# Two half loads of the first row block, and earlier turns of the second and third block, in a hybrid decoder layer

## The chip, the cores and the metric

The kernel runs on one core of one Trainium2 chip. The metric is the time of one execution on the device in microseconds (us), as the median of several runs. The engines are named as the profile names them: PE (TensorE, matrix products and transposes), PEld (its weight loads), DVE (VectorE), ACT (ScalarE), POOL (GpSimd) and SP (SyncE, which issues nearly all DMAs here).

## The reference

One decoder layer on `x` of 1024 rows by 1024 columns, in float32. The part that matters here is its very beginning: a normalised `x`, with a gain for each column, times a wide matrix `w_in`.

```python
h = rmsnorm(x, mix_pre_norm[layer])          # x * rsqrt(mean(x*x) + eps) * gain
proj = h @ w_in[layer]                       # 1024 x 1024 by 1024 x 3584
q_a, k_a, v_a, q_h, f_h, i_h, g_h = jnp.split(proj, splits, axis=-1)
...                                          # dilated attention, HGRN2 recurrence
mixed = jnp.concatenate([attn, rec], axis=-1) @ w_out[layer]
x = x + rmsnorm(mixed, mix_post_norm[layer])
h = rmsnorm(x, mlp_pre_norm[layer])
ff = jnp.square(jax.nn.relu(h @ w_ff1[layer])) @ w_ff2[layer]
x = x + rmsnorm(ff, mlp_post_norm[layer])
```

## The kernel before, in words

The rows of `x` are cut into eight blocks of 128 rows (`xrows[0]` to `xrows[7]`, tile `xr`), and its columns into eight pieces of 128 (`k` = 0 to 7). A product needs the transpose of each block, so each piece is *turned*. `x_turn(t0, n, k)` (lines 281 to 288) lets PE transpose piece `k` of `n` blocks into a PSUM bank (tile `xt`), ACT write the scaled result as the high part (tile `hTh`, line 287), and DVE write the rest that the high part has lost (tile `hTl`, line 288). The banks of the turns go round in a ring of four (two of tag `t`, two of tag `s`): a turn can only begin when DVE has read the turn four places before it.

Weights come in the same two parts. `first_half(i, c)` (line 315) splits half `c` (512 of 1024 columns) of the raw weights `raws[i]`: ACT writes the high part (`wig0h`, line 86), DVE the low part (`wig0l`, line 87). A product is three matrix products: high by high, high by low, low by high. The first products of the kernel use `raws[0]` and `raws[1]` together, since each product is 256 columns wide, 128 from either.

The stretch that the change touches is lines 333 to 369, an order written out by hand; every engine keeps to it.

1. `keep_warm` (line 307) multiplies zeros on PE while nothing has been loaded.
2. The eight turns of block 0 (`x_turn(0, 1, k)`), with small products of zeros between them. In ACT's and DVE's order, `first_half(0, 0)` stands behind turn 3, `first_half(1, 0)` behind turn 5, and `first_half(0, 1)` and `first_half(1, 1)` behind turn 7.
3. `x_firsts(0)`: the products of block 0 for `k` = 0 to 3 (eight with the high weights, then four with the low weights; helper `x_first`, line 321).
4. Four turns of block 1; then `x_firsts(1)`, the products of block 0 for `k` = 4 to 7.
5. A loop over the groups of blocks (1), (2,3), (4,5), (6), (7), in which the products of one group (`x_mm`, line 290) and the turns of the next alternate. `LAG` says how many turns of a group are left for the loop in which they are needed themselves.

All loads of this stretch are issued by SP in program order: block 0 of `x`, `raws[0]`, `raws[1]`, blocks 1 to 7 of `x`, two small tables, and from there each further weight block when its buffer is free. Behind the loop, ACT and DVE write out the products of the last groups (`ig_evac`), split two more weight blocks (`wh`, `wl`) and prepare masks, while PE begins the products `pm_q` and `pm_f`. From there a queue of pieces of work with written-out costs fills PE; nothing in that part is changed.

Of the kernel before, what the change touches and what calls it, by code (L numbers as in the profile page):

```python
# [17 lines left out]
P = 128  # L18
T = 1024
D = 1024  # L20
NK = D // P
# [11 lines left out]
def f32(ap):  # L33
    return ap.bitcast(F32)
# [3 lines left out]
def hymba_layer(ctx, tc, x, w_in, w_out, w_ff1, w_ff2, g_pre, lb_logits, g_mix, g_post,  # L38
                g_mlp, g_mlp_post, bias_tab, level_masks, ident_in, fold_in, out):
    nc = tc.nc  # L40
# [11 lines left out]
    def slab(tag, name, dtype=F32, shape=(P, T)):  # L52
        return sp.tile(list(shape), dtype, tag=tag, name=name,
                       bufs={"S": 9, "T": 9, "P": 3, "BT": 2, "V8": 2, "R": 1}[tag])

    def bank(tag, name):
        return ps.tile([P, 512], F32, tag=tag, name=name,
                       bufs={"mm": 2, "s": 2, "t": 2, "pv": 2}[tag])
# [21 lines left out]
    def rsqrt_mean(dst, ssum, n, width):  # L80
        t = col("ms", width)
        G.tensor_scalar(t, ssum, 1.0 / n, EPS, op0=ALU.mult, op1=ALU.add)
        G.tensor_tensor(out=dst, in0=t, in1=nhalf[:, :width], op=ALU.pow)
# [26 lines left out]
    def w_split(eng=V):  # L110
        i = done[1]
        if i < len(stream):
            if done[0] <= i:
                w_load()
            hl = stream[i][1]
            if hl is None:
                hl = (wp.tile([P, T], F32R, tag="wh", name=f"wh{i}", bufs=2),
                      wp.tile([P, T], F32R, tag="wl", name=f"wl{i}", bufs=2))
            else:
                hl = hl()  # L120
            raw = raws.pop(i)
            if WO0 <= i < W10:
                gain = gcols[:, i - WO0:i - WO0 + 1]
                S.activation(hl[0], raw, AF.Copy, scale=gain)
                eng.scalar_tensor_tensor(hl[1], raw, gain, f32(hl[0]), op0=ALU.mult, op1=ALU.subtract)
            else:
                split_into(hl[0], hl[1], raw, eng)
            parts[i] = hl
            done[1] += 1
            w_load()  # L130
# [34 lines left out]
    def ig_view(box, k):  # L165
        return tuple(box[q].rearrange("p j (k c) -> p j k c", k=NK)[:, :, k] for q in ("h", "l"))
# [58 lines left out]
    def part_tok(blk, k, t0, n=1):  # L225
        c = (t0 % 4) * P
        return tuple(blk[q, k // 4, t0 // 4][:, k % 4, c:c + n * P] for q in "hl")
# [6 lines left out]
    xrows = [slab("S", f"xr{t}") for t in range(NT)]  # L234

    def x_load(t):
        nc.sync.dma_start(out=xrows[t], in_=x[t * P:(t + 1) * P, :])
# [1 line left out]
    square = sp.tile([P, P], F32, tag="half", name="square", bufs=2)  # L239
    G.memset(square, 1.0)  # L240
    G.affine_select(ident, square, [[-1, P]], ALU.is_equal, 0.0, base=0, channel_multiplier=1)
    x_load(0)
    for _ in range(2):
        w_load()
    for t in range(1, NT):
# [13 lines left out]
    def ig_evac(hd, pm, blocks):  # L259
        for u, t in enumerate(blocks):  # L260
            S.activation(hd["inat"][:, t], pm[:, u, 0], AF.Copy, scale=rstd0[:, t:t + 1])
            V.tensor_scalar(hd["gate"][:, t], pm[:, u, 1], rstd0[:, t:t + 1], None, op0=ALU.mult)
# [18 lines left out]
    def x_turn(t0, n, k):  # L281
        hi, lo = part_tok(hT, k, t0, n)
        pt = bank("t" if turned[0] % 2 else "s", f"xt{t0}_{k}")[:, :n * P]
        turned[0] += 1
        for j in range(n):
            TE.transpose(pt[:, j * P:(j + 1) * P], xrows[t0 + j][:, k * P:(k + 1) * P], ident)
        S.activation(hi, pt, AF.Copy, scale=gpre[:, k:k + 1])
        V.scalar_tensor_tensor(lo, pt, gpre[:, k:k + 1], f32(hi), op0=ALU.mult, op1=ALU.subtract)

    def x_mm(t0, n, k):  # L290
        for t in range(t0, t0 + n):
            three_pass(place[t], part_tok(hT, k, t), ig_view(wig[0], k), k == 0, k == NK - 1)

    def squares(t0, n):
        for t in range(t0, t0 + n):
            dump = slab("P", f"sq{t}")
            S.activation(dump, xrows[t], AF.Square, accum_out=ssq0[:, t:t + 1])
# [9 lines left out]
    def keep_warm(n, w=256):  # L307

        for _ in range(n):
            TE.matmul(pms0[3].rearrange("p t j c -> p (t j c)")[:, :w], zero.to_broadcast([P, P]),  # L310
                      zero.to_broadcast([P, w]), start=True, stop=True)

    groups = ((0, 1), (1, 1), (2, 2), (4, 2), (6, 1), (7, 1))
# [7 lines left out]
    def x_first(k, w, q):  # L321
        TE.matmul(place[0], part_tok(hT, k, 0)[q], ig_view(wig[0], k)[w], start=k == w == q == 0,
                  stop=w == 1 and k == NK - 1)

    def x_firsts(c):
        ks = range(4 * c, 4 * c + 4)
        for k in ks:
            x_first(k, 0, 0)
            x_first(k, 0, 1)
        for k in ks:  # L330
            x_first(k, 1, 0)

    keep_warm(3)
    keep_warm(1, 128)
    for k in range(4):
        x_turn(0, 1, k)
    first_half(0, 0)
# [8 lines left out]
    for i in range(2):  # L346
        raws.pop(i)
        done[1] += 1
        w_load()
    x_firsts(0)  # L350
    for k in range(4):
        x_turn(*groups[1], k)
    x_firsts(1)
    LAG = 4
    for i, grp in list(enumerate(groups))[1:]:
        for k in range(NK):
            if i == 2 and k < LAG:
                x_turn(*grp, NK - LAG + k)
            if i == 1 and k < LAG:
                x_turn(*grp, NK - LAG + k)  # L360
            if i == 1 and k >= LAG:
                x_turn(*groups[2], k - LAG)
            elif 1 < i < len(groups) - 1:
                x_turn(*groups[i + 1], k)
            x_mm(*grp, k)
            if i in (2, 3) and k % 3 == 1:
                squares(3 * (i - 2) + k // 3, 1)
        if i == 3:
            rsqrt_mean(rstd0[:, :6], ssq0[:, :6], D, 6)
        if i == 4:  # L370
            ig_evac(heads[0], pms0[0], PAIRED[0])
            w_split()
            ig_evac(heads[0], pms0[1], PAIRED[1])
            squares(6, 2)
            rsqrt_mean(rstd0[:, 6:], ssq0[:, 6:], D, 2)
# [965 lines left out]
    for s in range(n_steps):  # L1341
        hd, i = divmod(s, 8)
# [959 lines left out]
```

## Time and profile before

| | |
|---|---|
| median of 3 runs | 1208.02 us (1207.78 to 1208.76) |
| the profiled execution, its own time | 1208.16 us |
| its span | 1206.1 us |
| around the span | 2.06 us |
| mean granted clock of PE | 0.999 |
| PE busy | 1195.9 us (99%) |
| DVE busy | 852.4 us (71%) |
| ACT busy | 548.9 us (46%) |

The span is the time from the first to the last recorded instruction. The share of busy time is an average over the whole kernel; the stretch in question is the first 40 us of 1206.

### The profile page before, as it was taken

The numbers are of one execution on the slowest core, as the hardware profiler recorded it, in microseconds if no ns is written. First come the engines' busy times: TensorE is split into PE (matmuls) and PEld (weight loads), VectorE is DVE, ScalarE is ACT, GpSimd is POOL, SyncE is SP. The second block draws the span as 40 slices with busy tenths as digits, with TensorE's granted clock in tenths as the row PEclk, the third lists the DMA queues.
The fourth block names the chain that finished last, engine by engine and source line by source line (L and its number), as shares of the span: only waits on it lengthen the run. The fifth ranks groups of instructions, "written<-read, shape, count | busy, mean of one in ns | idle before, by whom it ended". The sixth has DMA issues, their size and how long they took to land.

```text
span 1206.1 us, 17280 instructions
## 1 busy us (share of the span) xinstructions
PE 1195.9 (99%) x6342; PEld 1025.6 (85%) x6342; DVE 852.4 (71%) x1438; ACT 548.9 (46%) x1075; POOL 307.9 (26%) x290
## 2 busy tenths in 40 slices
PE   9999999999999999999999999999999999999998
PEld 8898989888888888888888888888888888888886
DVE  5696978776666768676689566766688553578796
ACT  7633333332565668755664222222234543434562
POOL 0121112021221210153321786575631000000022
PEclk9999999999999999999999999999999999999999
DMA  5222323123545456273514565554587534533337
GB/s 218 71 68 84 95 85 93 52 82 80 147 96 122 124 130 159 56 242 105 192 63 159 180 215 190 189 194 144 204 318 269 190 105 140 169 94 105 105 105 279
DMA packets 87091, 172.31 MB, mean 143 GB/s; under 512 B 14560, under 2 KB 40032, under 8 KB 87008
## 3 DMA queue, kind: packets, MB, share of 16 engines
q1 hardware_dynamic: 86864, 171.22, 44.3%
q8 instruction: 50, 0.82, 0.3%
q14 instruction: 33, 0.27, 0.1%
q10 hardware_dynamic: 144, 0.00, 0.0%
HBM read 116.91 MB, written 47.99 MB: 137 GB/s over the span
## 4 chain that ended last, share of the span: by engine, by line
PE 93%; DVE 2%; ACT 2%; issue 1%; DMA 0%; POOL 0%; DVEq 0%; POOLq 0%; ACTq 0%
PE f L2042 18%; PE f2s L2042 7%; PE pig L92 2%; PE pig L90 2%; PE pig L91 2%; PE pl L529 2%; PE pwo L90 2%; PE pwo L92 2%; PE pwo L91 2%; PE pm_ak L90 1%; PE pm_av L90 1%; PE pm_ak L92 1%; PE pm_ak L91 1%; PE pm_av L92 1%; PE pm_av L91 1%
## 5 line engine op out<-in xcount | busy, mean ns | idle before, releaser
L87 DVE TENSOR_TENSOR al<-ar,ah 128x1024 fp32r<-128x1024 f32 x56 | 70.6, 1260 | 80.5 <-ACT ah L86 78.2
L2042 PE MATMUL f<-bh,ah 128*128 128x512 f32 x320 | 124.5, 389 | 0.0
L2042 PE MATMUL f<-bl,ah 128*128 128x512 f32 x320 | 124.5, 389 | 0.0
L2042 PE MATMUL f<-bh,al 128*128 128x512 f32 x320 | 124.5, 389 | 0.0
L86 ACT ACTIVATE ah<-ar 128x1024 fp32r<-128x1024 f32 x56 | 59.1, 1056 | 86.9 <-DMA ar<-actd 83.3
L2042 PEld LDWEIGHTS f<-bh,ah 128*128 128x128 f32 x320 | 60.1, 188 | 12.6
L2042 PEld LDWEIGHTS f<-bh,al 128*128 128x128 f32 x320 | 60.1, 188 | 12.5
L2042 PEld LDWEIGHTS f<-bl,ah 128*128 128x128 f32 x320 | 60.1, 188 | 12.3
L2116 POOL TENSOR_SCALAR lbl<-ssq 128x1 f32<-128x1 f32 x4 | 3.3, 820 | 245.6 <-ACT fd L2112 245.5
L1665 POOL TENSOR_TENSOR e<-x,e 128x512 f32<-128x512 f32 x14 | 21.6, 1540 | 131.2 <-DVE x L1616 124.0
L2042 PE MATMUL f2s<-bl,ah 128*128 128x512 f32 (+1 forms) x128 | 48.9, 382 | 0.0
L2042 PE MATMUL f2s<-bh,al 128*128 128x512 f32 (+1 forms) x128 | 48.9, 382 | 0.0
L2042 PE MATMUL f2s<-bh,ah 128*128 128x512 f32 (+1 forms) x128 | 48.9, 382 | 0.0
L718 POOL TENSOR_SCALAR tout<-traw 128x256 f32<-128x256 f32 x16 | 18.4, 1149 | 109.2 <-DMA traw<-in_bias_tab_dram 93.4
L754 POOL TENSOR_TENSOR kl<-kf,kh 64x512 fp32r<-64x512 f32 x16 | 21.3, 1329 | 86.3 <-ACT kh L753 55.6
L87 DVE TENSOR_TENSOR bl<-br,bh 128x1024 fp32r<-128x1024 f32 x32 | 40.1, 1252 | 1.1 <-ACT bh L86 0.9
L2059 ACT ACTIVATE acc<-f 128x512 f32<-128x512 f32 x28 | 16.8, 598 | 49.6 <-PE f L2042 49.6
L802 POOL TENSOR_TENSOR ql<-qf,q 64x512 fp32r<-64x512 f32 x16 | 21.3, 1334 | 62.6 <-ACT q L801 62.0
L86 ACT ACTIVATE bh<-br 128x1024 fp32r<-128x1024 f32 x32 | 33.6, 1051 | 4.4 <-PE f L2042 3.1
L87 DVE TENSOR_TENSOR wl<-raw,wh 128x1024 fp32r<-128x1024 f32 x21 | 25.9, 1233 | 9.3 <-ACT wh L86 9.3
L90 PE MATMUL pwo<-woh,mt 128*128 128x512 f32 x80 | 32.2, 402 | 0.0
L92 PE MATMUL pwo<-woh,mt 128*128 128x512 f32 x80 | 31.3, 391 | 0.0
(1722 smaller groups left out, 3964.2 us busy)
## 6 DMA issues: line engine op xcount, KB each, us to landing
ar<-actd SPq DMA_DIRECT2D x56, 512.0 KB, 3.7
br<-in_w_ff_dram SPq DMA_DIRECT2D x16, 1024.0 KB, 6.2
raw<-in_w_in_dram SPq DMA_DIRECT2D x28, 512.0 KB, 4.0
w1r<-in_w_ff_dram SPq DMA_DIRECT2D x14, 1024.0 KB, 6.5
actd<-e SPq DMA_DIRECT2D x17, 768.0 KB, 4.3
actd<-e SPq DMA_DIRECT2D x11, 1024.0 KB, 4.1
xr<-in_x_dram SPq DMA_DIRECT2D x8, 512.0 KB, 8.3
raw<-in_w_out_dram SPq DMA_DIRECT2D x8, 512.0 KB, 3.6
```

The source lines that it names most:

```text
L86: S.activation(hi, src, AF.Copy)
L87: eng.tensor_tensor(out=lo, in0=src, in1=f32(hi), op=ALU.subtract)
L90: TE.matmul(dst, lhs[0], rhs[0], start=start, stop=False)
L91: TE.matmul(dst, lhs[0], rhs[1], start=False, stop=False)
L92: TE.matmul(dst, lhs[1], rhs[0], start=False, stop=stop)
L529: TE.matmul(pl[:, n % 2, :192], kt[:, n * P:(n + 1) * P], sets[u // 2][:, n % 4], start=True, stop=True)
L718: G.tensor_scalar(by_class(dst[:, part_ * w:(part_ + 1) * w]), in_blocks(raw[:, FAR * DIL:]), -1.0, None, op0=ALU.mult)
L754: G.tensor_tensor(out=kl[a:b], in0=src, in1=f32(kh[a:b]), op=ALU.subtract)
L802: G.tensor_tensor(out=by_class(lo[a:b]), in0=src, in1=by_class(f32(stacks[i]["q"][a:b, sl])), op=ALU.subtract)
L1665: eng[0].tensor_tensor(out=e1[:, 3], in0=a21, in1=e1[:, 2], op=ALU.add)
L2042: TE.matmul(pm, a[:, j, c], b[:, j, d], start=start and j == 0 and q == 0, stop=stop and j == 1 and q == 2, skip_group_check=True)
L2059: S.activation(acc_at(p, i), pm, AF.Copy)
```

## The change

Block 0 of `x` is loaded by two DMAs of 512 columns each instead of one of 1024. The last product of zeros ahead of the turns has 64 columns instead of 128. The first four turns of block 1 move from behind `x_firsts(0)` into it (behind its eight products with the high weights), and its other four turns move from the loop into `x_firsts(1)`, one ahead of each product with the low weights. In the loop, the turns of blocks 2 and 3 begin two steps sooner (`LAG` is 2 instead of 4).

```diff
-    x_load(0)
+    for c in range(2):
+        sl = slice(c * 512, c * 512 + 512)
+        nc.sync.dma_start(out=xrows[0][:, sl], in_=x[:P, sl])
     for _ in range(2):
         w_load()
...
             x_first(k, 0, 0)
             x_first(k, 0, 1)
         for k in ks:
-            x_first(k, 1, 0)
+            x_turn(*groups[1], k)
+            if c == 1:
+                x_first(k, 1, 0)
+        for k in ks:
+            if c == 0:
+                x_first(k, 1, 0)
 
     keep_warm(3)
-    keep_warm(1, 128)
+    keep_warm(1, 64)
...
     x_firsts(0)
-    for k in range(4):
-        x_turn(*groups[1], k)
     x_firsts(1)
-    LAG = 4
+    LAG = 2
     for i, grp in list(enumerate(groups))[1:]:
         for k in range(NK):
             if i == 2 and k < LAG:
-                x_turn(*grp, NK - LAG + k)
-            if i == 1 and k < LAG:
                 x_turn(*grp, NK - LAG + k)
             if i == 1 and k >= LAG:
                 x_turn(*groups[2], k - LAG)
```

## Rows read from the trace of the kernel before

**Rows 1.** The page: busy time, its share of the span, and instructions of PE.

```profile
PE 1195.9 (99%) x6342; PEld 1025.6 (85%) x6342; DVE 852.4 (71%) x1438; ACT 548.9 (46%) x1075; POOL 307.9 (26%) x290
```

**Rows 2.** Stretches: length, busy time by engine, granted PE clock, DMA share, GB/s.

```profile
8.14:37.30 29.16, 29.16 (x248) 29.16 (x249) 18.71 (x49) 24.11 (x60) 1.57 (x2) 1.00 0.37 146
1197.00:1199.00 2.00, 2.00 (x19) 2.00 (x18) 1.51 (x3) 0.47 (x2) 0.45 (x1) 1.00 1.02 393
4.90:6.20 1.30, 1.28 (x6) 1.23 (x6) 0.40 (x2) 0.80 (x4) 0.00 (x0) 1.00 1.04 419
```

**Rows 3.** The chain of work that ended last, first 60 us: start, length, what.

```profile
0.79 3.99 DMA xr<-in_x_dram
...
7.57 0.53 ACT wig0h L86
8.14 1.69 PE pig L322 x12
...
34.13 0.12 PE xt L286
34.28 0.38 ACT hTh L287
```

**Rows 4.** Timeline of PE: start, length, instruction, idle before it and releaser.

```profile
3.69 0.63 PE L310 MATMUL pig<-zero 128*128 128x128 f32 x2
4.92 1.09 PE L286 MATMUL xt<-ident,xr 128*128 128x128 f32 x4 [0.59 <-DMA xr<-in_x_dram]
5.79 0.63 PE L310 MATMUL pig<-zero 128*128 128x128 f32 x2
7.25 0.60 PE L310 MATMUL pig<-zero 128*128 128x256 f32 x2
8.14 0.38 PE L322 MATMUL pig<-wig0h,hTh 128*128 128x256 f32 x1 [0.30 <-ACT wig0h L86]
9.19 0.64 PE L322 MATMUL pig<-wig0l,hTh 128*128 128x256 f32 x4
9.67 0.60 PE L286 MATMUL xt<-ident,xr 128*128 128x128 f32 x4
10.03 0.37 PE L322 MATMUL pig<-wig0h,hTh 128*128 128x256 f32 x1
11.06 0.64 PE L322 MATMUL pig<-wig0l,hTh 128*128 128x256 f32 x4
```

**Rows 5.** Timeline of SP: the DMA issues.

```profile
1.23 0.42 SPq L107 DMA_DIRECT2D raw<-in_w_in_dram  x1
1.70 0.42 SPq L107 DMA_DIRECT2D raw<-in_w_in_dram  x1
2.17 4.23 SPq L237 DMA_DIRECT2D xr<-in_x_dram  x7
```

**Rows 6.** DMA issues: first load of weights; second; block 1 of `x`. KB, us to landing.

```profile
raw<-in_w_in_dram SPq DMA_DIRECT2D x1, 512.0 KB, 4.8
raw<-in_w_in_dram SPq DMA_DIRECT2D x1, 512.0 KB, 5.6
xr<-in_x_dram SPq DMA_DIRECT2D x1, 512.0 KB, 6.4
```

**Rows 7.** Timeline of ACT, columns as for PE.

```profile
5.40 1.14 ACT L287 ACTIVATE hTh<-xt,gpre 128x128 fp32r<-128x128 f32 x4 [2.68 <-PE xt L286]
6.41 0.64 ACT L86 ACTIVATE wig0h<-raw 128x512 fp32r<-128x512 f32 x1
6.93 0.64 ACT L287 ACTIVATE hTh<-xt,gpre 128x128 fp32r<-128x128 f32 x2
7.43 0.66 ACT L86 ACTIVATE wig0h<-raw 128x512 fp32r<-128x512 f32 x1
```

**Rows 8.** Timeline of DVE, columns as for PE.

```profile
8.82 0.61 DVE L288 SCALAR_TENSOR_TENSOR hTl<-xt,gpre,hTh 128x128 fp32r<-128x128 f32 x2
10.54 1.12 DVE L288 SCALAR_TENSOR_TENSOR hTl<-xt,gpre,hTh 128x128 fp32r<-128x128 f32 x4
```

## The prediction

> **What bounds the kernel now.** I read the page first, then the stretches, then the chain of waits, and last the timelines of single engines in the first 12 us. The page gives PE 99% of the span [rows 1], so a change can only win where PE is not at work, or where it works too slowly. The stretches show that PE has no gap from 8.14 us on, where the first product starts, to 37.3 us: 29.16 us busy of 29.16, at granted clock 1.00 [rows 2]. The moved turns all lie in that stretch. So a new order of the same PE work can't win there; it can only open gaps. What is left to win lies ahead of 8.14 us, where PE transposes eight pieces and otherwise multiplies zeros.
>
> What sets 8.14 us? The chain of waits runs from the load of block 0 (3.99 us from 0.79, so it lands at 4.78) to an ACT split of weights at 7.57, and from there to the first product at 8.14 [rows 3]. Between the two lies ACT: four evacuations of turns from 5.40, the split of the first weights from 6.41, two more evacuations from 6.93, the split of the second weights from 7.43, each starting as the one ahead of it ends [rows 7]. The first product needs both splits, and PE idles 0.30 us ahead of it until the second is done [rows 4]. Read alone, this chain says: let block 0 land sooner and everything moves up. But the splits have a second input, the weights. Those are issued at 1.23 and 1.70 us [rows 5] and take 4.8 and 5.6 us [rows 6], so they land at 6.03 and 7.30. From a landing to the start of the engine that waited for it are 0.14 us (4.78 to 4.92 on PE [rows 3, 4]). The second weights can be used from 7.44 us; ACT uses them from 7.43. They have no slack at all. This pair of numbers decides the case.
>
> **The halved load.** From 4.9 to 6.2 us the DMAs move 419 GB/s at a full share [rows 2]. Half of 512 KB is 262,144 B, which takes 0.63 us, so the first half should land at about 4.15. Its bounds: no earlier than the whole (4.78), if the halves come in together, and half of the 3.99 us at best. PE could not use that best case, since its products of zeros end at 4.32 (3.69 + 0.63 [rows 4]), now cut by half of the last one's two records, some 0.21 us, to 4.11; so PE starts its turns between 0 and 0.81 us sooner, and I take 0.63.
>
> What the head start is worth: ACT's four evacuations begin at 4.77 instead of 5.40, and the first split could start at 5.78 instead of 6.41. The first weights land at 6.03 and count from 6.17, so 0.24 us is won there. After that the two evacuations (0.5 us to the next start) end in time for the second split at 7.19, and there ACT stands and waits for weights that count from 7.44. The gain at the first product is 7.43 - 7.44: nothing. The same bytes stand ahead of the second weights as before.
>
> What the load costs: rows of 2 KB instead of 4 KB. The stores at the end, 2 KB rows too, move 393 GB/s at a share of 1.02, against 419 at 1.04 [rows 2]; on 524,288 B that is 1.33 against 1.25 us, about 0.08 us later for all that follows. SP issues one DMA more, and all later ones slip by a slot: from 0.79 to 1.23 and to 1.70 are 0.44 and 0.47 us [rows 3, 5]. As long as the DMA engines have a backlog, that is hidden: the second weights take 5.6 us from issue to landing, and only about 1.25 us of that is their own transfer. Without this cover the slot costs 0.47 us. I take 0.08, with 0 and 0.47 as ends.
>
> The Trainium skill (DMA: Bandwidth & Descriptors, Bandwidth) would price it higher: its table, measured for loads issued from GpSimd, gives 0.95 us for 64 KB and 6.15 us for 1 MB, and advises batches of 1 MiB. On the line between these, my estimate is 2.0 us for each half and 3.4 us for the whole, so 0.6 us of loss; the stores in this trace, at 393 GB/s, speak against it where transfers queue up.
>
> **The moved turns of block 1.** Today they run at 9.67 and take 0.36 us up to the next product at 10.03, about 0.11 with the dearer switch back counted [rows 4]. Now four stand at 9.19, behind the eight high products. Their input, block 1, is issued at 2.17 [rows 5] and takes 6.4 us [rows 6]: 8.57, hidden by 0.6 us. Their banks: the third and fourth need DVE done with turns 6 and 7 of block 0, which end at about 9.16 and 9.43 [rows 8]; PE reaches them at 9.41 and 9.52. The four low products then run 0.44 us later, and `x_firsts(1)` starts at 10.03 as before. Its eight high products end at 11.06 [rows 4]; then turns 4 to 7 of block 1 alternate with the low products, at 11.06, 11.29, 11.52 and 11.75. They need DVE done with turns 0 to 3 of block 1. DVE does these from 10.54 in 1.12 us [rows 8], because it splits the second halves of the weights first, and that doesn't change: ends at about 10.88, 11.14, 11.40, 11.66. The margins are 0.18, 0.15, 0.12 and 0.09 us. No stall, but tight: if DVE ran 0.2 us later against PE, each turn would wait once, some 0.1 us in all. I take 0; the ends are 0 and 0.3.
>
> **The moved turns of blocks 2 and 3.** They begin with the third step of the loop instead of the fifth. PE's work is the same number of instructions, so the loop ends where it did. Blocks 2 and 3 follow block 1 at 1.25 us each: about 9.8 and 11.1, used from some 12.7. ACT is busy 24.11 of 29.16 us there and DVE 18.71 [rows 2], so the evacuations have room. Cost 0.
>
> **What carries on.** From 34.13 the chain goes from the last turn into ACT [rows 3], so what ACT and DVE write out afterwards hangs on PE's order as PE itself does: a shift at 8.14 arrives at the end in full, neither grown nor lost.
>
> **The sum.** Gain at the first product 0.0; the 2 KB rows +0.08; stalls 0. So the second weights count from about 7.52, ACT starts the split 0.09 later than 7.43, and the end is some 0.1 us later. The profiled execution took 1208.16 us (span 1206.1 and 2.06 around it), 0.14 above the median of 1208.02; I forecast 1208.1 for a median. A change of 0.2% is 2.4 us, about what a measurement of this kernel can tell from no change; everything summed so far is far below that.
>
> **The rivals.** *The head start goes through*: the second weights are not what holds the split, since a wait ended by a DMA isn't shown there, and the two small loads ramp up faster and bring all that follows forward. At most the whole 0.63 us arrives: 1207.4. For it speaks the chain of waits, which names only the load of block 0 and ACT; against it the 7.30 landing. *The weights come later*: the extra issue is not covered early on, and the second weights land up to 0.47 us later: 1208.5, with stalls at the tight banks 1208.8. For it speaks that the backlog has only begun to build when these loads are issued. This is also how the skill's advice to batch would show, at about the size estimated above. *The change does nothing it says*: the first half lands with the second, and ACT starts as before; 1208.1 too, for the same reason.
>
> *Slower for sure*: PE's clock. The four transposes from 4.92 take 0.87 us to the next operation, 0.22 each; the four from 9.67 take 0.36, 0.09 each [rows 4]. The first is the level of 1.2 GHz, the second that of 2.4, though the granted clock of the row from 4.90 says 1.00 [rows 2]. PE had worked on zeros up to 4.32, then paused 0.59 us, before it rose. Now PE begins its turns sooner, has fewer zeros to multiply, and is done with them at about 7.2 instead of 7.85 (7.25 + 0.60), while the product still starts past 8.1: it idles about a microsecond there instead of 0.30. If the clock is at the low level when the products start, the 24 products to 11.98 take about 0.21 instead of 0.12 us each and the eight turns 0.22 instead of 0.11: 2.2 + 0.9 = 3.1 us, 1211.2. It decides only if the low level lasts through nearly all of that stretch; half of it gives 1.5. Against it: PE will have worked longer without the 0.59 us pause. The Trainium skill (TensorE: Matmul & The Clock Gate, Part 1) calls the slow clock the default and says that activity releases it; nothing here shows a fall.
>
> **How the numbers follow.** My forecast 0.50, and 0.08 for a change that does nothing at the same time; the head start 0.18; the later weights 0.19; the clock 0.05. The likeliest time is 1208.1. To hold 8 in 10, the range takes in the head start and the later weights and leaves out the clock; with some 0.2 us for the scatter of a median it is 1207.2 to 1209.0. Faster by over 0.2% would need more than the whole head start: 0.02. Slower by over 0.2% needs most of the clock's case: 0.03. The rest, 0.95, is the same.
>
> **What the new profile would show.** The first turn on PE at about 4.3 instead of 4.92; ACT's first split at about 6.2 and a gap on ACT ahead of the second, ended by the weights, at about 7.5; the first product between 8.1 and 8.3; turns of block 1 at about 9.2 and 11.1 with no wait for a bank; PE unbroken from there. I am wrong if the first product starts before 7.9 or after 8.7, or if PE's products in the first microseconds behind it stand 0.21 us apart.

## The result, and the profile after

The changed kernel takes 1210.83 us in the median of 15 runs (1208.56 to 1212.41), the kernel before, run beside it, 1207.95 (1207.78 to 1208.76, 15 runs). The ratio is 1.0020 with a 95% interval of 1.0013 to 1.0027: slower by 2.9 us, at about the bound that the prediction set for a difference, and outside its range. The runs also scatter over 3.9 us instead of 1.0. Seven of them show a mean granted clock of 0.999 and a median of 1209.41; eight show 0.996 to 0.998 and a median of 1211.06. So there are two losses to look for: one that all runs have, and one that comes and goes with the clock.

The profiled execution took 1210.02 us and is one of the first seven. Its page: PE's busy time is the same within 0.3 us, so the loss is idle time of PE.

```profile
span 1208.1 us, 17284 instructions
...
PE 1195.6 (99%) x6342; PEld 1025.6 (85%) x6342; DVE 854.0 (71%) x1438; ACT 548.7 (45%) x1075; POOL 308.4 (26%) x290
```

PE's timeline, columns as in [rows 4] (`keep_warm` is now line 312, the turns 288, `x_first` 324):

```profile
4.01 1.06 PE L288 MATMUL xt<-ident,xr 128*128 128x128 f32 x4
...
6.30 0.60 PE L312 MATMUL pig<-zero 128*128 128x256 f32 x2
10.17 0.39 PE L324 MATMUL pig<-wig0h,hTh 128*128 128x256 f32 x1 [3.26 <-ACT wig0h L86]
...
11.23 0.60 PE L288 MATMUL xt<-ident,xr 128*128 128x128 f32 x4
11.58 0.72 PE L324 MATMUL pig<-wig0l,hTh 128*128 128x256 f32 x4
...
13.10 0.27 PE L288 MATMUL xt<-ident,xr 128*128 128x128 f32 x1
13.12 0.37 PE L324 MATMUL pig<-wig0l,hTh 128*128 128x256 f32 x1
...
13.79 0.27 PE L288 MATMUL xt<-ident,xr 128*128 128x128 f32 x1
```

The head start is there: the first turn runs at 4.01 instead of 4.92 [rows 4]. Then PE is out of work at 6.90 and idles 3.26 us, and the first product starts at 10.17 instead of 8.14: 2.03 us later, which is the 2.0 us by which the span has grown. From there PE stands nowhere; no moved turn has a wait behind it. ACT's timeline, against [rows 7]:

```profile
4.47 1.14 ACT L289 ACTIVATE hTh<-xt,gpre 128x128 fp32r<-128x128 f32 x4 [1.75 <-PE xt L288]
8.23 0.63 ACT L86 ACTIVATE wig0h<-raw 128x512 fp32r<-128x512 f32 x1 [2.62 <-DMA raw<-in_w_in_dram]
8.77 0.61 ACT L289 ACTIVATE hTh<-xt,gpre 128x128 fp32r<-128x128 f32 x2
9.48 0.63 ACT L86 ACTIVATE wig0h<-raw 128x512 fp32r<-128x512 f32 x1
```

ACT evacuates turns 0.93 us sooner and then waits 2.62 us for the first weights. The second split, at 9.48, shows no wait, but the chain of waits, followed back from it, does not go to ACT's own work before it, but to a load:

```profile
2.17 7.29 DMA raw<-in_w_in_dram
9.48 0.64 ACT wig0h L86
10.17 1.22 PE pig L324 x8
```

The second weights were issued at 2.17 instead of 1.70 [rows 5] and landed at 2.17 + 7.29 = 9.46 instead of 7.30. Only 0.47 of these 2.16 us is the later issue; the transfer itself took 7.3 instead of 5.6 us. The stretches show why (columns as in [rows 2]; the last column is GB/s). First before:

```profile
4.00:8.00 4.00, 3.26 (x20) 2.52 (x19) 2.04 (x7) 2.60 (x9) 0.00 (x0) 1.00 1.02 414
4.00:7.30 3.30, 2.71 (x19) 2.38 (x19) 1.34 (x5) 1.90 (x7) 0.00 (x0) 1.00 1.02 415
```

and the same of after, the second up to its own landing:

```profile
4.00:8.00 4.00, 2.90 (x20) 2.35 (x19) 1.12 (x4) 1.14 (x4) 0.00 (x0) 1.00 0.94 317
4.00:9.46 5.46, 2.90 (x20) 2.35 (x19) 1.69 (x5) 2.29 (x7) 0.00 (x0) 1.00 0.97 344
```

At a busy share of 0.94, so nearly always at work, the 16 DMA engines move a quarter less per second. Up to the landing they moved 3.30 x 415 = 1370 KB before and 5.46 x 344 = 1878 KB after. At the old rate the 1878 KB would have taken 4.53 us: 0.93 of the 2.16 us is the rate. The other 508 KB at 415 GB/s are the remaining 1.22: bytes of later loads, moved while a part of the second weights was still owed. The Trainium skill (DMA: Bandwidth & Descriptors, Why a DMA increments its semaphore by 16 and not by 1) says that the engines of one DMA finish independently and that it has landed only with the last of them; these 508 KB agree with it, though no row here tells the 16 engines apart.

The records of single packets in the trace carry the lower rate. Packets of 4 KB (a row of weights) that begin from 4 to 8 us:

```
                     packets   median   over 250 ns   longest
before                  404    159 ns        2          324 ns
after                   310    159 ns       30         1471 ns
```

The typical packet is as fast as before; one in ten is not. What they have beyond 159 ns is 0.68 us for each of the 16 engines (before: 0.03).

### The profile page after: what moved, and what is told of

The parts are those of the page before. It is cut to its first block, busy times and chain, and to the rows that moved or that the text cites. A ratio compares the mean times of both kernels' runs of the same rounds, so it can differ in the third digit from the quotient of the medians.

```text
span 1208.1 us, 17284 instructions
## 1 busy us (share of the span) xinstructions
PE 1195.6 (99%) x6342; PEld 1025.6 (85%) x6342; DVE 854.0 (71%) x1438; ACT 548.7 (45%) x1075; POOL 308.4 (26%) x290
## 4 chain that ended last, share of the span: by engine, by line
PE 94%; DVE 2%; ACT 1%; issue 1%; DMA 1%; POOL 0%; SPq 0%; DVEq 0%; POOLq 0%; ACTq 0%
PE f L2045 18%; PE f2s L2045 7%; PE pig L90 2%; PE pig L92 2%; PE pig L91 2%; PE pl L532 2%; PE pwo L90 2%; PE pwo L92 2%; PE pwo L91 2%; PE pm_q L90 1%; PE pm_q L92 1%; PE pm_q L91 1%; PE pm_ak L90 1%; PE pm_av L90 1%; PE pm_ak L92 1%; PE pm_ak L91 1%
```

## The experiments

The kernel before was run beside every group of them; its medians were 1207.86 to 1208.08 us, its slowest single run 1209.89. The theory at first: the two half loads bring the weights late, the order costs nothing, and the clock makes some runs worse. The rivals: the 2 KB packets, the moved turns, and a first touch of the weights' memory.

**Halves alone, order alone.** The kernel before with only the two half loads, and the change with block 0 in one load:

```diff
-    x_load(0)
+    for c in range(2):
+        sl = slice(c * 512, c * 512 + 512)
+        nc.sync.dma_start(out=xrows[0][:, sl], in_=x[:P, sl])
```

> Only the load of block 0 in two halves of its columns; zeros and order of the turns as before. If the load makes the loss (the weights then land near 8.2 and 9.5 us instead of 6.0 and 7.3), the time is 1209 to 1212 and scatters as after the whole change. If the moved turns make it, the time is 1207.5 to 1208.2, with little scatter.

> Only the moved turns and the shorter product of zeros; block 0 loaded whole. If the load makes the loss, the weights land at 6.0 and 7.3 us, the first product starts at about 8.1, and the time is 1207.8 to 1208.2. If the moved turns make it, the time is 1209 to 1211 with gaps on PE between 9 and 12 us.

Halves alone: 1210.63 us (1208.62 to 1211.36, 11 runs), ratio 1.0020 (1.0010 to 1.0029). Order alone: 1207.77 (1207.66 to 1209.22, 11 runs), 0.9999 (0.9991 to 1.0008). The halves are the whole loss. The profiled run of the halves (1210.63) has the other loss too. PE's timeline:

```profile
9.26 0.40 PE L324 MATMUL pig<-wig0h,hTh 128*128 128x256 f32 x1 [1.95 <-ACT wig0h L86]
9.48 0.39 PE L324 MATMUL pig<-wig0h,hTl 128*128 128x256 f32 x1
9.67 0.42 PE L324 MATMUL pig<-wig0h,hTh 128*128 128x256 f32 x1
...
13.13 0.28 PE L324 MATMUL pig<-wig0h,hTl 128*128 128x256 f32 x1
13.26 0.28 PE L324 MATMUL pig<-wig0h,hTh 128*128 128x256 f32 x1
```

and its stretches:

```profile
6.39:9.80 3.41, 1.46 (x10) 1.06 (x10) 1.78 (x4) 2.37 (x7) 0.00 (x0) 0.96 1.01 387
9.80:13.22 3.42, 3.42 (x19) 3.42 (x18) 2.41 (x8) 1.92 (x6) 0.00 (x0) 0.55 1.03 419
13.22:16.60 3.38, 3.38 (x31) 3.38 (x30) 1.89 (x7) 1.74 (x6) 0.00 (x0) 1.00 1.03 401
```

PE idles 1.95 us and the first product is 1.1 us late. Then the granted clock falls to 0.55, nearly the level of 1.2 GHz, and products stand 0.21 us apart; at 13.13 they stand 0.13 apart again, the level of 2.4. The span is 2.6 us longer than that of before: 1.1 from the late weights, 1.5 from the clock.

**Row halves; halves on two queues.** Two loads of 64 rows, so that the packets keep 4 KB; and the first column half issued by ACT, the second by SP, so that the weights keep their slots of 1.23 and 1.70 us:

```diff
+        rs = slice(c * 64, c * 64 + 64)
+        nc.sync.dma_start(out=xrows[0][rs, :], in_=x[rs, :])
...
+    nc.scalar.dma_start(out=xrows[0][:, :512], in_=x[:P, :512])
     nc.scalar.dma_start(out=gpre, in_=g_pre)
...
-    x_load(0)
+    nc.sync.dma_start(out=xrows[0][:, 512:], in_=x[:P, 512:])
```

> As before, but block 0 loaded by two DMAs of 64 rows each with whole rows of 4 KB, so the weights are issued one slot (0.47 us) later and the packets keep their size. If the later issue of the weights makes the loss, they land near 8 and 9.3 us and the time is 1209 to 1212. If the 2 KB rows make it, the weights land at about 6.0 and 7.3 and the time is 1207.8 to 1208.3.

> As before, but block 0 in two halves of its columns, the first issued by ACT at about 0.8 us and the second by SP at 0.8, so that the weights are issued at 1.23 and 1.70 as before while the packets are 2 KB. If the later issue of the weights makes the loss, it is gone: the weights land at about 6.0 and 7.3, the time is 1207.5 to 1208.3. If the 2 KB rows make it, it stays: 1209 to 1212.

Row halves: 1209.56 us (1209.20 to 1211.59, 11 runs), 1.0017 (1.0008 to 1.0026), 301 GB/s from 4 to 8 us, with packets of 4 KB in both loads. So 2 KB packets are not needed for the loss. The weights were later here than in the change, though: each load of 64 rows took SP 0.6 us to issue, and they left at 2.06 and 2.68 us instead of 1.71 and 2.17. Two queues: 1209.03 (1208.86 to 1211.14, 11 runs), 1.0013 (1.0004 to 1.0021). That miss is of my making. ACT's timeline:

```profile
6.15 1.14 ACT L288 ACTIVATE hTh<-xt,gpre 128x128 fp32r<-128x128 f32 x4 [2.94 <-DMA gpre<-in_g_pre_dram]
```

The gains `gpre`, 4 KB, the one load of this stretch that ACT issues, were now issued behind a half load, at 1.23 us instead of 0.79, and took 4.8 us to land instead of 4.2 as in the profile of before; the evacuations waited for them. The DMA engines moved 412 GB/s in this run and the weights landed at 5.8 and 7.1, no later than before. As a test of the loss it says only that half loads as such don't slow the DMA engines. But this run (1209.88 us) has a fall of the clock, with the weights in time, behind two pauses of PE (0.43 us for block 0 and 1.39 for a bank):

```profile
7.60:10.90 3.30, 3.30 (x16) 3.07 (x16) 3.14 (x9) 2.80 (x8) 0.00 (x0) 0.50 1.03 410
```

**Second half by ACT; late weights; weights between.** Halves from SP and ACT again, with the gains kept first on ACT and its first small activation moved behind the issue; the kernel before with a whole load, but the first weights held back by a POOL `memset` of a part of their buffer, so that they issue at 1.66 and 2.04; and the two halves with the first weights between them:

```diff
+    nc.sync.dma_start(out=xrows[0][:, :512], in_=x[:P, :512])
+    nc.scalar.dma_start(out=xrows[0][:, 512:], in_=x[:P, 512:])
...
+            if i == 0:
+                G.memset(raws[i][:, :256], 0.0)
...
+    for c in range(2):
+        sl = slice(c * 512, c * 512 + 512)
+        nc.sync.dma_start(out=xrows[0][:, sl], in_=x[:P, sl])
+        w_load()
```

> As before, but block 0 in two halves of its columns, the first issued by SP at 0.8 us, the second by ACT behind its load of the gains; the weights are issued at 1.23 and 1.70 as before. If the third place in SP's queue is what delays the weights, they land at about 5.9 and 7.1 us at over 400 GB/s, and the time is 1207.4 to 1208.0. If small first transfers are enough to slow the DMA engines, the rate from 4 to 8 us falls to 250 to 350 GB/s and the time is 1209 to 1211.

> As before, block 0 whole, but the first load of weights waits for a small POOL write of its buffer (0.4 us or so), so that the weights are issued later without any more DMAs. If a later issue of the weights behind block 0 is enough, the DMA rate falls from 4 to 8 us, the weights land at 7.5 us or later and the time is 1209 to 1211. If it takes one more DMA in front of them, the rate stays above 400 GB/s, the weights land within 0.4 us of 6.0 and 7.3, and the time is 1207.8 to 1208.4.

> As before, but block 0 in two halves of its columns with the first weights issued between them: half, weights, half, weights, all by SP. The first weights are issued at 1.23, the second at about 2.15. If it is the later issue of both weights, the first land at about 5.4 and the second at 7.3, and the time is 1207.6 to 1208.3. If one more DMA near the front of SP's queue is enough, whatever stands where, the rate falls as after the change and the time is 1209 to 1212.

Second half by ACT: 1207.90 us (1207.78 to 1209.51, 11 runs), 0.9997 (0.9988 to 1.0006). The loss is gone, with half loads, and the rate is back. Its stretch:

```profile
4.00:8.00 4.00, 3.46 (x19) 3.19 (x19) 2.43 (x7) 2.97 (x9) 0.00 (x0) 1.00 1.03 416
```

The profiled run (1209.51 us) is the slowest of the 11; the others took 1207.78 to 1208.21. PE's timeline has something else in it, with the weights in time:

```profile
6.15 0.45 PE L287 MATMUL xt<-ident,xr 128*128 128x128 f32 x1 [0.54 <-DVE hTl L289]
...
9.70 0.41 PE L323 MATMUL pig<-wig0h,hTh 128*128 128x256 f32 x1
9.91 0.41 PE L323 MATMUL pig<-wig0h,hTl 128*128 128x256 f32 x1
...
10.33 0.28 PE L323 MATMUL pig<-wig0h,hTl 128*128 128x256 f32 x1
10.44 0.64 PE L323 MATMUL pig<-wig0l,hTh 128*128 128x256 f32 x4
```

Up to about 10.1 us products stand 0.21 us apart, the level of 1.2 GHz, from 10.33 on 0.11 to 0.12. So the first rise of the clock came late here; before it PE had paused 0.54 us. The low products start at 10.44 instead of 9.19 [rows 4]: 1.25 of the 1.35 us by which this run is slower than the profiled run of before (1208.16). The granted clock of that stretch reads 1.00 and the run's mean 0.999: neither shows a first rise that comes late.

Late weights: 1208.54 (1207.92 to 1209.14, 11 runs), 1.0001 (0.9992 to 1.0010). The interval does not tell it from no change, but the profile has a small copy of the loss without any half load: 362 GB/s, 16 packets over 250 ns, the longest 1326 ns. ACT's timeline:

```profile
8.13 0.63 ACT L86 ACTIVATE wig0h<-raw 128x512 fp32r<-128x512 f32 x1 [0.95 <-DMA raw<-in_w_in_dram]
```

Weights between: 1208.40 (1207.73 to 1210.32, 11 runs), 1.0003 (0.9994 to 1.0012), 401 GB/s, second split at 7.23. It has as many DMAs on SP as the change and issues the second weights as late, at 2.17. So neither the number of DMAs nor the slot of the second weights makes the loss; the slot of the first weights may.

**A first touch.** If the first reads of the weights' memory were what is slow, touching it early should help. The change with two small DMAs on ACT, issued at 0.79 and 1.23, that read 64 B of each row of the two weight blocks; as a control the same of rows of `w_ff2`, which nothing reads early:

```diff
+    touch = cp.tile([P, 2, 16], F32, name="touch")
+    for i in range(2):
+        nc.scalar.dma_start(out=touch[:, i], in_=w_in[i][:, :16])
     nc.scalar.dma_start(out=gpre, in_=g_pre)
```

> The changed kernel, with two tiny DMAs by ACT ahead of its load of the gains, each reading 64 B of every row of one of the two weight blocks into a tile that nothing uses. If the slow packets are first reads of memory not yet touched, they are gone: no fall of the rate from 4 to 8 us, the second weights land at about 7.3 to 7.6 and the time is 1207.7 to 1208.5. If the memory's state has no part in it, the time is 1209 to 1212 as after the change.

> The control of the run before: the same two tiny DMAs, but from rows of another weight matrix that is needed much later. If first reads are the cause, the time stays at 1209 to 1212; if the tiny DMAs help by something else (their small packets between the large ones), it is as low as in the run before.

1211.68 us (1210.45 to 1212.40, 6 runs) and 1211.87 (1211.42 to 1213.19, 5 runs), ratios 1.0030 (1.0018 to 1.0041) and 1.0034 (1.0021 to 1.0046). In both profiles the weights take 6.5 and 7.3 us to land, as in the profile after, though the touching reads had landed by 4.5 us, ahead of most of the weights' packets. So nothing speaks for the theory. Both are slower still because the gains, behind the small DMAs on ACT's queue, land 6.6 and 6.7 us after their issue.

**A version to beat both.** The kernel before with the second half by ACT and the weights in column halves, the two first halves first:

```diff
+    for c in range(2):
+        for i in range(2):
+            sl = slice(c * 512, c * 512 + 512)
+            nc.sync.dma_start(out=raws[i][:, sl], in_=stream[i][0][:, sl])
```

> The order of the kernel before, with block 0 in two halves of its columns (the first by SP, the second by ACT) and each of the two weight blocks in two halves too, the halves that are needed first ahead of the others. If the landing of the second weights is what holds the first product, their first half lands near 5, ACT runs without a wait from 4.5 us, the first product starts at about 7.2 instead of 8.1 and the time is 1207.0 to 1207.5. If the later place of the loads slows the DMA engines here too, the rate from 4 to 8 us falls and the time is 1208.3 to 1210.

PE's timeline of its profiled run (1207.42 us):

```profile
7.33 0.39 PE L328 MATMUL pig<-wig0h,hTh 128*128 128x256 f32 x1 [0.17 <-ACT wig0h L86]
```

The first product comes 0.81 us sooner than in the profile of before, but the median is 1207.82 (1207.42 to 1208.18, 11 runs), 0.9999 (0.9990 to 1.0008). A gain under 1 us at this place can't be told from none; it doesn't beat the kernel before.

**The whole change, first weights by ACT.** The change with one thing undone, the later issue: ACT issues the first weights at 1.22 (its first small activation again behind that), SP the second at 1.70.

```diff
-            nc.sync.dma_start(out=raws[i], in_=stream[i][0])
+            (nc.scalar if i == 0 else nc.sync).dma_start(out=raws[i], in_=stream[i][0])
```

> The whole change, but the first weights are issued by ACT behind the gains, at about 1.23 us, so that the second weights follow the two halves on SP at 1.71: both weights leave as early as before the change. If their later issue is what costs the time, the rate from 4 to 8 us stays near 400 GB/s, the second weights land at about 7.3 and the time is 1207.6 to 1208.4. If two small loads in a row on SP's queue cost it, whoever issues the weights, the time stays at 1209 to 1212.

> The whole change, but block 0 in four loads of 256 columns, so that the weights are issued at about 2.6 and 3.1 us, two more slots later. If the later issue is the cause, the loss grows: the second weights land at 10 us or later and the time is 1210.5 to 1213. If any split costs a fixed disturbance, the time is 1209 to 1212 as with two halves.

First weights by ACT: 1207.96 us (1207.86 to 1209.90, 11 runs), 1.0006 (0.9997 to 1.0015), 405 GB/s, weights landed at 5.9 and 7.4, first product at 8.10. The loss of the change is gone in the median; the interval still allows for 1.8 us. Its stretch, and PE's timeline:

```profile
4.00:8.00 4.00, 2.65 (x20) 2.08 (x19) 2.34 (x7) 2.88 (x9) 0.00 (x0) 1.00 1.01 405
```

```profile
8.10 0.39 PE L324 MATMUL pig<-wig0h,hTh 128*128 128x256 f32 x1 [0.98 <-ACT wig0h L86]
```

The other kernel of this group is the change with four loads of 256 columns, weights issued at 2.65 and 3.12: 1211.41 (1209.43 to 1212.30, 6 runs), 1.0027 (1.0015 to 1.0038). Each quarter lands in 2.2 to 2.5 us, but two more slots do not cost clearly more than one: the second weights landed at 9.0, and the first product ran at 9.72.

**Zeros in the gap; block 1 ahead.** The change with four more products of zeros behind the last turn, so that PE goes on working until shortly before the first product; and the kernel before with block 1 ahead of the weights, which are then issued as late as in the change (1.70 and 2.17), but behind 1024 KB instead of 512:

```diff
+    keep_warm(4)
     for i in range(2):
         first_half(i, 1)
...
     x_load(0)
+    x_load(1)
     for _ in range(2):
         w_load()
-    for t in range(1, NT):
+    for t in range(2, NT):
```

> The whole change, with four more products of zeros of 256 columns behind the last turn of block 0, so that PE idles some 1.7 us less ahead of the first product. If the slow executions of the changed kernel (1210.8 to 1212.4) are those in which TensorE's clock falls after the idle time, they are gone: mean granted clock 0.999 in nearly all runs, times of 1208.5 to 1210.2, median about 1209.5. If the late weights alone make the whole spread, the times stay at 1208.6 to 1212.4 with a median near 1210.8.

> As before the change, with block 1 of x issued ahead of the two weight blocks: the weights are issued at about 1.7 and 2.2 us as after the change, but behind 1024 KB instead of 512. Without a fall of the rate the weights land one transfer of 1.25 us later, at about 7.3 and 8.6, and the first product starts at about 9.4. If a thin queue ahead of the weights makes the rate fall, it stays above 400 GB/s from 4 to 8 us here, and the time is 1209.0 to 1209.6 where the clock holds. If the late issue of the weights itself does it, the rate is 300 to 360 GB/s, the weights land at 9 us or later, and the time is 1210 to 1213.

Zeros in the gap: 1209.56 us (1208.91 to 1209.97, 11 runs), 1.0012 (1.0003 to 1.0020). All 11 runs show a mean granted clock of 0.999 or more, and the worst run is better than the median of the change. PE's timeline:

```profile
6.49 2.34 PE L312 MATMUL pig<-zero 128*128 128x256 f32 x10
9.24 0.39 PE L324 MATMUL pig<-wig0h,hTh 128*128 128x256 f32 x1 [0.41 <-ACT wig0h L86]
9.46 0.28 PE L324 MATMUL pig<-wig0h,hTl 128*128 128x256 f32 x1
9.58 0.28 PE L324 MATMUL pig<-wig0h,hTh 128*128 128x256 f32 x1
```

The weights are as late as in the profile of the halves alone (320 GB/s), the products stand 0.12 us apart. Block 1 ahead: 1209.15 (1209.03 to 1211.18, 10 runs), 1.0012 (1.0003 to 1.0021). Its stretch, and ACT's timeline:

```profile
4.00:8.00 4.00, 3.02 (x20) 2.16 (x19) 1.39 (x5) 2.07 (x7) 0.00 (x0) 1.00 1.03 421
```

```profile
8.36 0.63 ACT L86 ACTIVATE wig0h<-raw 128x512 fp32r<-128x512 f32 x1
```

Full rate, one packet over 250 ns; the split is 0.93 us later than in [rows 7] and the first product 0.91 later than in [rows 4], less than the 1.25 us that 512 KB more take at that rate. So a late issue alone does not slow the DMA engines. All 16 kernels side by side, by what SP and ACT had asked for (the gains and the small touching reads left out) ahead of 1.6 us:

```
                          KB asked for    GB/s,      second weights   median
                          by 1.6 us       4 to 8 us  land, us         us
quarters                    256             341          9.0          1211.41
change                      512             317          9.5          1210.83
halves alone                512             337          8.6          1210.63
row halves                  512             301          9.0          1209.56
zeros in the gap            512             320          8.6          1209.56
late weights                512             362          8.1          1208.54
weights between             768             401          7.2          1208.40
before                     1024             414          7.3          1207.95
second half by ACT         1024             416          7.2          1207.90
first weights by ACT       1024             405          7.4          1207.96
order alone                1024             417          7.0          1207.77
block 1 ahead              1024             421          8.4          1209.15
weights touched             512             300          9.5          1211.68
other memory touched        512             284          9.5          1211.87
weights in halves           768             385          7.5          1207.82
two queues                 1024             412          7.1          1209.03
```

In the last four rows the second weights are not what the first product waited for: the gains were late in three, and the weights in halves needed only their first half, landed at 6.2. The bound of 1.6 us was chosen after the runs. The kernels divide nearly the same way by whether a load of 512 KB was issued at about 1.23 us (all of those with 401 GB/s or more); no run parts the two readings.

## Why the prediction was wrong, point by point

**What bounds the start: right.** The second weights decide when the first product runs, before, after and in most of these profiles; so the head start, which is real (4.01 and 4.47 us), is worth nothing. My bound for it was too narrow, to no effect: I took 0.63 us for the first turn and 0.81 at most, and it gained 0.91. And "no slack at all" was misread by a little: I took PE's 0.14 us from a landing to its start for ACT too, but ACT began its split 0.02 us behind the landing of the second weights in the profile after (9.46 and 9.48). Before, they had some 0.1 us of slack.

**The step that failed: "As long as the DMA engines have a backlog, that is hidden".** I counted the cost of the half loads at 0.08 us, all of it the 2 KB rows, and the extra issue at nothing, with 0.47 as the upper end, one slot. The second weights landed 2.16 us later in the profile after, some 1.25 in those of the halves alone and of the zeros. The rival that stood against it ("the backlog has only begun to build when these loads are issued") named the right place, and it was priced as a shift by one slot. What the runs show in its place: in the kernels that have asked for no more than 512 KB by 1.6 us, the rate from 4 to 8 us is 284 to 362 GB/s instead of 401 to 421 (385 with the weights in halves), and the weights land late. In the profile after, single packets of these 4 us take up to 1.47 us instead of 0.16. The first weights issued early put this right with the rest of the change in place (1207.96); a load of 1024 KB ahead of equally late weights shows no fall (421 GB/s); a late issue behind a whole load of 512 KB shows part of it (362). Without the clock's part the loss in the median is 1209.56 - 1207.95 = 1.6 us.

**The 2 KB rows: right that they cost little.** Half loads of 2 KB rows ran beside 405 to 416 GB/s with the second half or the first weights by ACT, and the loss is there with 4 KB rows. The price from the Trainium skill (DMA: Bandwidth & Descriptors, Bandwidth), an estimate of 2.0 us for each half and so 0.6 us of loss, is not borne out as a cost of half loads: two kernels with them lie within their intervals of before, and in the profile after the halves landed 2.9 and 3.0 us after their issue where the whole took 3.99 [rows 3]. Its direction, fewer and larger loads, was right for this change.

**The moved turns: right.** Order alone is at 0.9999. In the profile after, the turns at 11.23 and from 13.10 to 13.79 run without a wait, and so they do in the profile of order alone, where the first product ran at 7.71, so that no late weights gave DVE more time. The margins of 0.09 to 0.18 us held.

**What carries on: right.** 2.03 us at the first product became 2.0 us of span.

**The clock: named, priced and then dismissed.** I gave it 0.05, because PE "will have worked longer without the 0.59 us pause", and thought of about a microsecond of idling. With the weights late, PE idles 2 to 3.3 us. In the profile of the halves alone the clock stands at the low level for most of the first products and costs 1.5 us, the "half of it" that I had priced. For the change itself no trace shows it, since its profiled run kept the clock. But eight of 15 runs have a lower mean and are 1.7 us slower in the median, and zeros in the gap take it away in 11 of 11: 1210.83 - 1209.56 = 1.3 us of the median. A mean over 1208 us given to a thousandth is a coarse measure of 3 us at half speed: of the ten profiles here whose mean reads 0.998, five show a fall (halves alone, two queues, both with touching reads, quarters) and five do not, so the count of eight is rough. The falls stand behind idle time of PE, whatever it waited for: with two queues the weights were in time, and the clock fell too. Idle time alone doesn't settle it, since 3.26 us of it in the profile after had no fall behind it. And some scatter is neither: in the run with the late first rise (second half by ACT) the low products came 1.25 us later than before. The Trainium skill (TensorE: Matmul & The Clock Gate, Part 1) calls the number of slow products at a kernel's start run-variable; this late rise agrees with it. Whether a fall behind a gap varies for the same reason, no run here shows.

So of the 2.9 us some 1.6 are late weights and 1.3 the clock, which fell while PE waited for them. This parting is by medians; in single profiles the late weights put off the first product by 1.1 us (halves alone, zeros in the gap) to 2.0 (after). I had both as rivals and treated them as independent.

**What stays open.** Why single packets take so long when little is queued ahead. Not the packet size, the moved turns, untouched memory, the number of DMAs, or a late issue by itself: each of these was varied and the loss did not follow it. The bytes asked for early do go with the rate in all the kernels of the table, but within the group of 512 KB the rate runs from 284 to 362 and the least (256) has 341, each from one profile. It is an order, not a law, and what happens inside the DMA engines was not seen.

## What to carry to other kernels

Before a load is split to start sooner, look for the second input of whoever uses it: if that one has no slack, the head start is worth nothing, and each issue put ahead of it is a risk. At the start of a kernel, issue large loads early and let a second queue take the extra ones; don't reckon a late issue as a shift by one slot before a trace shows the rate behind it. And when a change makes PE wait ahead of a block of products, the wait can be paid twice: put work into the gap and compare, and look at the granted clock and at the scatter of single runs, since one profile may show only one of the cases.

## What was not expected of the hardware

The DMA engines, busy at 0.94 of the time, moved 317 instead of 414 GB/s in the same 4 us of two kernels that load the same data, because one packet in ten took 0.25 to 1.47 us where the others took 0.16. And a small DMA can be held up by what was asked for ahead of it, on its own queue and on the other: as ACT's first DMA, 4 KB of gains landed some 0.2 us behind SP's first load in 12 of 13 profiles (2.4 to 4.2 us after their issue; in the row halves 1.6), 4.8 us after it behind a half load of 256 KB, and 6.6 behind two reads of 8 KB in rows of 64 B.
